# A transformer layer on one Trainium2 core: deferred down products, norm chains in pieces on VectorE, five slabs ahead and three equal token groups

## The chip, the core and the metric

The kernel is one launch on one core of a Trainium2 chip. The core has a matrix engine (TensorE, PE in the profile; PEld are its weight loads), three engines for element work (VectorE, DVE; ScalarE, ACT; GpSimd, POOL) and a queue that starts most transfers (SyncE, SP). Each engine executes its own instructions in the order in which they were written; they wait for one another by semaphores. The metric is the time of one execution on the device in microseconds; the kernel before takes 1278.63 us (median of three runs, 1278.6 to 1278.74).

## The reference, cut to what matters

One layer of a hybrid decoder, float32 in and out, 1024 prompt tokens and 32 sample tokens, T = 1056 columns in all, model width 1024:

```python
h = _rms(x, n_mix_pre)
z = h @ w_in                                   # q, k, v, pooling inputs
a, k_state, v_state = attn_fn(q, k, v)          # sliding window of 128, sinks
m, pool_state = _pool_mixer(u, pool_prev, pos0, w_pool, pool_scale)
mix = jnp.concatenate([a, m], axis=-1) @ w_out
x = x + _rms(mix, n_mix_post)
f = _rms(x, n_ffn_pre)
f = (jax.nn.silu(f @ w_gate) * (f @ w_up)) @ w_down     # D_FF = 2816
x = x + _rms(f, n_ffn_post)
x = x + jax.nn.sigmoid(x @ w_ple_gate) * (p @ w_ple)
```

`_rms(x, g)` is x / sqrt(mean(x*x) + 1e-6) * g over the model width. The states of the caches are outputs too.

## The kernel before

Activations lie transposed: the model width on 128 partitions in 8 pieces (KC), the tokens along the columns. The tokens are cut into three groups g = 0, 1, 2 of `NS` = 384, 384 and 288 columns. A tensor of one group is kept as two halves of 4 pieces (`half`, 128 x 4 x NS[g]).

**Precision by splits.** Each operand of a large product is kept as a high part, cast by ScalarE (`wh`, `fh`, `hid`, `sh`), and the rest, subtracted by VectorE (`wl`, `fl`, `sl`); the function is `split`. A product of one 128 x 128 weight piece is three matmuls: high x high, high x low, low x high (`gemm`). `ops8` is a product over all 8 pieces, so 24 matmuls; `ops4` over 4, so 12. Raw weights come by SP's queue into `wr` tiles (`W_RAW` = 2 buffers), and the split pairs into a ring of `W_PAIRS` = 4 pairs. A tile is reused when TensorE has read it for the last time; a cast that needs it waits for that.

**Stages.** First norm and input projection; pooling and attention, filled up with out-projection products; the rest of the out-projection; then the feed-forward part; then the last stage (`ple_out`), the gate and projection of the per-layer input. The feed-forward width is 22 chunks of 128, two chunks a slab, 11 slabs. For each slab and the groups that take part, `gate_up` makes gate and up of each chunk and puts silu(gate) * up, split, into `hid`; `down` multiplies by the slab's rows of `w_down` and adds to the outputs `o` on VectorE.

**Seven products.** Groups 0 and 1 go together through gate and up by seven products instead of eight, with sums of the weights (`w_sums`: four GpSimd operations and two splits into `sh`, `sl`, called S1 to S4) and sums of the operands (`t_sum`, T1 to T4). Their first two products, of the gate's own weights with B11 and B21, need no sum; the third needs S2. Group 2 takes direct products (`direct`, 24 matmuls each).

**WALK.** It is the list of (slab, groups): `AHEAD` = 3 slabs of group 2 alone, then 8 slabs of all three, then the first 3 slabs of groups 0 and 1 alone. While group 2 works alone, the norms of groups 0 and 1 are made. A group's chain (`ffn_steps`) is: sum of squares over partitions on TensorE (`acc`), root on ScalarE, `dg` on VectorE, a matmul that spreads the factor r over the partitions, y*r on VectorE, x+y on GpSimd, squares on ScalarE, sums of the halves (`sum_halves`) on GpSimd and VectorE, the second norm's factor in the same way, eight scalings by gain and r on VectorE (`scalar_tensor_tensor`), two operand splits. `ple_steps` is the chain behind the last down products. The chains are generators whose three or four parts are called between products at fixed places.

**Order.** TensorE's instructions stand in the order of the code; the downs of a slab follow its two chunks directly. What the other engines do stands in an order that a scheduler makes from the code's order and its own estimates of readiness.

Of the kernel before, what the change touches and what calls it, by code (L numbers as in the profile page):

```python
# [16 lines left out]
P = 128  # L17
# [7 lines left out]
NS = (384, 384, 288)  # L25
OFF = (0, 384, 768, T)
G = 3
NX = max(NS)
# [8 lines left out]
AHEAD = 3  # L37
# [9 lines left out]
W_RAW = 2  # L47


A_SLOTS, B_SLOTS = 20, 7  # L50
# [3 lines left out]
def trunk_kernel(  # L54
# [47 lines left out]
    def big(shape, dt=F32, s="a"):  # L102
        return apool.tile(shape, dt, tag="a", bufs=A_SLOTS, name=nm(s))

    def small(shape, dt=F32, s="b"):
        return apool.tile(shape, dt, tag="b", bufs=B_SLOTS, name=nm(s))

    def half(g, dt=F32, s="h", home=None):
        return (home or (small if g == 2 else big))([P, 4, NS[g]], dt, s)

# [80 lines left out]
    WALK += [(s, (0, 1)) for s in range(AHEAD)]  # L191
    WGU, WD = [], []
    for s, _ in WALK:
        WGU.append([[add_plan(w_gu[c, j], [P, KC, P]) for j in range(2)] for c in range(SLAB * s, SLAB * s + SLAB)])
        WD.append([add_plan(w_dn[s, j], [P, SLAB, 512]) for j in range(2)])
    WPE = []
    for _ in range(2):
        w = []
        for m in range(KC):
            if m % 4 == 0:  # L200
                wp = add_plan(w_ple[m // 4], [P, 2, 512])
            w.append((wp, add_plan(w_pg[m], [P, KC, P])))
        WPE.append(w)

# [16 lines left out]
    def rstd_steps(acc):  # L221
# [4 lines left out]
        w = n // G  # L226
        sm = bank()
        for i in range(G):
            mm(sm[:w, i : i + 1], acc[:, i * w : (i + 1) * w], ones[:, 0:1], start=True, stop=True)
        sd = spool.tile([P, G], F32, tag="sd", name=nm("sd"))  # L230
        se.activation(sd[:w], sm[:w, :G], AF.Sqrt, bias=epst[:w], scale=1.0 / D)
# [4 lines left out]
            ident[:w, :w].unsqueeze(1).to_broadcast([w, G, w]),  # L236
            sd[:w].unsqueeze(2).to_broadcast([w, G, w]),
            op=ALU.mult,
        )
        yield  # L240
# [15 lines left out]
    def sum_halves(sqs, g, eng):  # L256

        a, b = sqs
        eng.tensor_tensor(a, a, b, op=ALU.add)
# [10 lines left out]
    for g in range(G):  # L270
# [19 lines left out]
        acc1.append(sum_halves(sqs, g, ve))  # L290
# [11 lines left out]
    wpl2 = small([P, 2, 4, P], F32R)  # L302
    wplh, wpll = wpl2[:, 0], wpl2[:, 1]
    split(wplh, wpll, wpl)
    sts = big([P, 8 * NDEC * PST + 4 * 16 + 4 * PST])
# [19 lines left out]
    def u_proj(c):  # L325
        w = weights(U0[c])
        ue = big([P, ULEN])
# [17 lines left out]
        two = [big([P, ULEN]) for _ in range(min(2, c + 1))]  # L345
# [30 lines left out]
    qkv = [big([P, T]) for i in range(6)]  # L376
# [11 lines left out]
    misc = big([P, 6, P])  # L388
# [11 lines left out]
    vtok = big([P, NB, P])  # L400
# [599 lines left out]
```

## Time and profile before

| | us |
|---|---|
| median of three runs | 1278.63 |
| profiled execution | 1280.9 |
| its span, first to last instruction | 1279.1 |
| TensorE busy in the span | 1161.9 |
| VectorE / ScalarE / GpSimd busy | 729.3 / 428.0 / 243.6 |
| mean granted clock of TensorE | 0.951 |
| start, to the first uninterrupted work of TensorE | 0 to 57.3 |
| group 2 alone in its first slabs | 305.8 to 446 |
| slabs of all three groups | 446 to 965 |
| slabs of groups 0 and 1 alone | 965 to 1129.6 |
| last downs and turn to the last stage | 1129.6 to 1172.9 |

The clock is the share of full speed that TensorE was granted. A row of a window gives for each engine its busy time and the number of instructions, then that clock, the busy share of the DMA engines and their rate. A row of a group names the line, the engine, the operation, output and inputs, shapes, the count, then busy us and mean ns. A row of waits gives the total, the number and the longest.

### The profile page before, as it was taken

How to read it: one execution, taken by the hardware profiler on the slowest of the kernel's cores; microseconds unless marked ns; L12 is line 12 of the kernel's file. 1: busy time of each engine (PE TensorE's matmuls, PEld its weight loads, DVE VectorE, ACT ScalarE, POOL GpSimd, SP SyncE). 2: the span in 40 equal slices, each digit the busy share in tenths (PEclk: the TensorE clock that was granted, in tenths of full speed). 3: DMA queues.
4: the chain of work that ended last, by engine and by line, in shares of the span. 5: the costliest groups of instructions: out<-in, count | busy, mean ns of one | idle time of the engine just before them, and what ended most of it. 6: DMA issues, size and time to landing. Idle time of an engine off the chain costs nothing.

```text
span 1279.1 us, 17291 instructions
## 1 busy us (share of the span) xinstructions
PE 1161.9 (91%) x7075; PEld 1121.9 (88%) x7075; DVE 729.3 (57%) x1117; ACT 428.0 (33%) x744; POOL 243.6 (19%) x180
## 2 busy tenths in 40 slices
PE   4599998998947799999999999999999798968998
PEld 3499985788946799999999999999999698968998
DVE  7655245753558745364646464656566856597432
ACT  5222045554446324321313132323232322354220
POOL 3343021124450021111111121202021111100000
PEclk8699998998978899999999999999999899987999
DMA  5211120062233212011202021212112112225421
GB/s 202 66 34 61 41 103 18 17 238 84 82 115 99 100 33 67 33 67 34 67 34 66 34 66 34 67 33 67 34 67 79 66 50 66 83 98 183 146 87 44
DMA packets 33375, 94.80 MB, mean 74 GB/s; under 512 B 3956, under 2 KB 14484, under 8 KB 33296
## 3 DMA queue, kind: packets, MB, share of 16 engines
q1 hardware_dynamic: 31536, 91.93, 21.1%
q10 hardware_dynamic: 1760, 1.78, 0.4%
q8 instruction: 55, 0.90, 0.3%
q14 instruction: 24, 0.20, 0.1%
HBM read 83.58 MB, written 10.11 MB: 73 GB/s over the span
## 4 chain that ended last, share of the span: by engine, by line
PE 59%; DVE 7%; issue 1%; ACT 1%; DMA 1%; POOL 0%; DVEq 0%; ACTq 0%; POOLq 0%
PE b L115 59%; DVE fl L145 1%; DVE x L842 1%; DVE wl L145 1%; DVE y L673 1%; DVE acc L565 0%; POOL wr L714 0%; DMA wr<-in_w_dn_dram 0%; DVE sl L145 0%; ACT sh L144 0%; DVE o L839 0%; DVE y L643 0%; ACT wh L144 0%; DVE hid L145 0%; DMA wr<-in_w_gu_dram 0%
## 5 line engine op out<-in xcount | busy, mean ns | idle before, releaser
L115 PE MATMUL b<-hid,wh 128*128 128x384 f32 (+1 forms) x1056 | 258.5, 330 | 25.3 <-ACT hid L144 17.8
L115 PE MATMUL b<-fh,wh 128*128 128x288 f32 (+1 forms) x808 | 257.2, 318 | 0.0
L115 PE MATMUL b<-fh,wl 128*128 128x288 f32 (+1 forms) x808 | 256.2, 317 | 0.0
L115 PE MATMUL b<-fl,wh 128*128 128x288 f32 (+1 forms) x808 | 256.2, 317 | 0.0
L144 ACT CAST wh<-wr 128x1024 fp32r<-128x1024 f32 x128 | 134.0, 1048 | 267.6 <-PE b L115 221.1
L145 DVE TENSOR_TENSOR wl<-wr,wh 128x1024 fp32r<-128x1024 f32 x128 | 172.4, 1348 | 83.0 <-ACT wh L144 83.0
L115 PEld LDWEIGHTS b<-hid,wh 128*128 128x128 f32 x1056 | 189.4, 193 | 29.3 <-ACT hid L144 19.3
L714 POOL TENSOR_TENSOR wr<-wr 128x512 f32<-128x512 f32 x44 | 62.3, 1415 | 599.7 <-DVE wl L145 598.0
L115 PE MATMUL b<-hid,wl 128*128 128x384 f32 (+1 forms) x528 | 172.7, 327 | 1.2 <-DVE wl L145 1.2
L810 DVE TENSOR_TENSOR o<-o,b 128x384 f32<-128x384 f32 (+1 forms) x240 | 121.2, 518 | 63.6 <-PE b L115 62.6
L115 PEld LDWEIGHTS b<-fh,wh 128*128 128x128 f32 x808 | 154.6, 191 | 0.3
L115 PEld LDWEIGHTS b<-fl,wh 128*128 128x128 f32 x808 | 154.4, 191 | 0.3
L115 PEld LDWEIGHTS b<-fh,wl 128*128 128x128 f32 x808 | 154.3, 191 | 0.0
L115 PE MATMUL b<-h,wh 128*128 128x384 f32 (+1 forms) x480 | 119.5, 335 | 17.0 <-ACT wh L144 10.2
L144 ACT CAST sh<-wr 128x1024 fp32r<-128x1024 f32 x44 | 46.0, 1048 | 234.1 <-PE b L115 170.3
L115 PE MATMUL b<-fh,sl 128*128 128x384 f32 x352 | 118.8, 337 | 2.3 <-DVE sl L145 2.3
L115 PE MATMUL b<-fh,sh 128*128 128x384 f32 x352 | 118.7, 337 | 2.2 <-ACT sh L144 2.2
L115 PE MATMUL b<-fl,sh 128*128 128x384 f32 x352 | 118.3, 336 | 0.0
L115 PEld LDWEIGHTS b<-h,wh 128*128 128x128 f32 x480 | 88.1, 198 | 18.1 <-ACT wh L144 10.2
L115 PEld LDWEIGHTS b<-hid,wl 128*128 128x128 f32 x528 | 102.0, 193 | 1.5 <-DVE wl L145 1.5
L145 DVE TENSOR_TENSOR sl<-wr,sh 128x1024 fp32r<-128x1024 f32 x44 | 53.8, 1223 | 74.2 <-ACT sh L144 74.2
L115 PE MATMUL b<-h,wl 128*128 128x384 f32 (+1 forms) x240 | 79.7, 333 | 2.7 <-DVE wl L145 2.7
(157 smaller groups left out, 1658.1 us busy)
## 6 DMA issues: line engine op xcount, KB each, us to landing
wr<-in_w_gu_dram SPq DMA_DIRECT2D x56, 512.0 KB, 3.2
wr<-in_w_dn_dram SPq DMA_DIRECT2D x28, 512.0 KB, 3.2
wr<-in_w_pg_dram SPq DMA_DIRECT2D x16, 512.0 KB, 3.5
wr<-in_w_in_dram SPq DMA_DIRECT2D x10, 512.0 KB, 3.4
wr<-in_w_out_b_dram SPq DMA_DIRECT2D x8, 512.0 KB, 3.3
xr<-in_x_dram SPq DMA_DIRECT2D x4, 768.0 KB, 6.9
wr<-in_w_out_a_dram SPq DMA_DIRECT2D x6, 512.0 KB, 3.2
x<-in_x_dram SPq DMA_DIRECT2D x4, 768.0 KB, 8.6
```

The costliest lines, as they stand in the source:

```text
L115: ins = te.matmul(*args, **kw)
L144: se.copy(hi, src)
L145: ve.tensor_tensor(lo, src, hi.bitcast(F32), op=ALU.subtract)
L673: ve.tensor_tensor(out, a, b, op=ALU.subtract)
L714: ge.tensor_tensor(out, a, b, op=op)
L810: ve.tensor_tensor(o, o, v, op=ALU.add)
L842: ve.scalar_tensor_tensor(xh[:, c, :], yh[:, c, :], gn[:, 3, k : k + 1], xh[:, c, :], op0=ALU.mult, op1=ALU.add)
```

## The change

The token groups become three of 352. The chains get all their additions on VectorE and are cut into smaller pieces; `turn` counts matmuls and lets a chain's next piece out when VectorE should have done the one before (`load / share`). `AHEAD` is 5, so that `WALK` has 5 slabs of group 2, 6 of all groups, 5 of groups 0 and 1. The down products of a slab are issued behind the next slab's first products, and for all groups alternately. The last stage begins with two tiles of group 2 ahead of the last downs. Weights are asked for through one list of items in the order of use (`need`, four items ahead), raw buffers are 3. One pool of 27 slots replaces two of 20 and 7. The attention blocks go 5, 6, 7, 0 to 4 instead of 6, 7, 0 to 5.

```diff
-NS = (384, 384, 288)
-OFF = (0, 384, 768, T)
 G = 3
-NX = max(NS)
+N = T // G
+NS = (N,) * G
+TB = 4
-AHEAD = 3
+AHEAD = 5
+LOOK = 4
-W_RAW = 2
-A_SLOTS, B_SLOTS = 20, 7
+W_RAW = 3
+A_SLOTS = 27
...
+    def need(k, ahead=LOOK):
+        for i in range(len(made), min(k + ahead + 1, len(ITEMS))):
+            kind, js = ITEMS[i]
+            if kind == "direct":
+                w_split(js[0])
+                made[i] = pairs[js[0]]
+            else:
+                made[i] = w_sums(*(raws[ITEMS[j][1][0]] for j in js))
+            for kind, js in ITEMS[i + 1 : i + 3]:
+                if kind == "direct":
+                    w_load(js[0])
+        return made[k]
...
-            eng.tensor_tensor(acc_g, acc_g, sq, op=ALU.add)
+            ve.tensor_tensor(acc_g, acc_g, sq, op=ALU.add)
...
+    def turn(n, share=0.45):
+        now[0] += n
+        for ch in list(chains):
+            while ch in chains and ch[1] <= now[0]:
+                try:
+                    load, wait = next(ch[0])
+                except StopIteration:
+                    chains.remove(ch)
+                    break
+                dve[0] = max(dve[0], now[0]) + load / share
+                ch[1] = dve[0] + wait
...
         for yh, xh in zip(ys[g], x1[g]):
             ve.tensor_tensor(yh, yh, bc4(r), op=ALU.mult)
-            ge.tensor_tensor(xh, xh, yh, op=ALU.add)
+            ve.tensor_tensor(xh, xh, yh, op=ALU.add)
             se.activation(yh, xh, AF.Square)
-        acc2 = sum_halves(ys[g], g, ge)
-        yield
+            yield 20, 0
+        yield 0, 13
+        acc2 = sum_halves(ys[g], g)
+        yield 20, 6
...
+        wg = need(ig)
+        if 0 in gs:
+            p1 = tmp(n, "p1")
+            se.copy(p1, product(quarter(wg, 0), f7["B11"]))
+        if 2 in gs:
+            sl = tmp(n, "sl")
+            se.activation(sl, direct(wg), AF.Silu)
+        if 0 in gs:
+            c11 = tmp(n, "c11")
+            add(c11, p1, product(quarter(wg, 1), f7["B21"]))
+            se.activation(c11, c11, AF.Silu)
+        if pending:
+            pending()
...
+    def downs(n):
+        s, gs = WALK[n]
+        for m in range(KC):
+            for g in (2, 0, 1):
+                if g in gs:
+                    (last_down if g == 2 and s == NSLAB - 1 else down)(n, m, g)
+        if s == NSLAB - 1:
+            chain(ple_steps(2), 19)
     for n, (s, gs) in enumerate(WALK):
...
         for i in range(SLAB):
-            gate_up(*WGU[n][i], i, gs, between)
...
+            gate_up(WGU[n][i], i, gs, (lambda: downs(n - 1)) if i == 0 and n else None)
...
+    for m in range(FIRST):
+        ple_out(0, m, 2)
+    for m in range(KC):
+        last_down(END, m, 0)
+    chain(ple_steps(0), 19)
+    for m in range(KC):
+        last_down(END, m, 1)
+    chain(ple_steps(1), 19)
+    for m in range(FIRST, KC):
+        ple_out(0, m, 2)
```

How this stands in the engines' own orders is shown at three places. The first is VectorE at the end of the out-projection, before slab 0. In these rows y_1263 and y_2531 (before), y_1266 and y_2532 (after) belong to group 0, y_1265 and y_2181 (before), y_1268 and y_2188 (after) to group 2; fl_2606, and in the change fl_2831 and fl_2840, are the low parts of group 2's operands, and dg is what the factor is made from. Before:

```order
L145 TENSOR_TENSOR wl_2525<-wr_2522,wh_2524 128x1024
L232 RECIPROCAL sd_2564<-sd_2564 96x3
L234 TENSOR_TENSOR dg_2567<-c_76,sd_2564 96x288
L643 SCALAR_TENSOR_TENSOR y_1265<-x_2315,c_72,b_2598 128x288 x4
L643 SCALAR_TENSOR_TENSOR y_2181<-x_2317,c_72,b_2598 128x288 x3
L145 TENSOR_TENSOR fl_2606<-y_1265,fh_2605 128x1152
L643 SCALAR_TENSOR_TENSOR y_2181<-x_2317,c_72,b_2598 128x288
```

And in the change:

```order
L277 TENSOR_TENSOR dg_2781<-c_76,sd_2778 88x352
L704 TENSOR_TENSOR y_1266<-y_1266,b_2818 128x1408
L608 TENSOR_TENSOR acc_1303<-acc_1303,sq_2809 128x352
L147 TENSOR_TENSOR wl_2813<-wr_2736,wh_2812 128x1024
L705 TENSOR_TENSOR x_2326<-x_2326,y_1266 128x1408
L716 SCALAR_TENSOR_TENSOR y_1268<-x_2322,c_72,b_2823 128x352 x4
L716 SCALAR_TENSOR_TENSOR y_2188<-x_2324,c_72,b_2823 128x352 x3
L147 TENSOR_TENSOR fl_2831<-y_1268,fh_2830 128x1408
L716 SCALAR_TENSOR_TENSOR y_2188<-x_2324,c_72,b_2823 128x352
L704 TENSOR_TENSOR y_2532<-y_2532,b_2818 128x1408
L147 TENSOR_TENSOR fl_2840<-y_2188,fh_2839 128x1408
L705 TENSOR_TENSOR x_2328<-x_2328,y_2532 128x1408
```

Group 0's y*r and x+y now stand between group 2's second dg and the splits of group 2's operands. On TensorE the two factors stand together at the very end of the out-projection (b_2783 is its last product), right ahead of slab 0:

```order
L117 MATMUL b_2783<-mh_187,wl_2526 128x352
L117 MATMUL b_2818<-dg_2701,c_81 128x352
L117 MATMUL b_2823<-dg_2781,c_81 128x352
L117 MATMUL b_2850<-fh_2830,wh_2685 128x352
L117 MATMUL b_2850<-fl_2831,wh_2685 128x352
```

Before, six out-projection products stood between the factor of group 2 (made from dg_2567) and slab 0.

The second place is ScalarE in a slab of groups 0 and 1 alone, at its second chunk (p is the first product, c becomes silu of the second, sh are the casts of the weight sums):

```order
L829 COPY p_8705<-b_8706 128x352
L836 ACTIVATE c_8720<-c_8720 128x352
L146 CAST sh_8695<-wr_8396 128x1024
L146 CAST sh_8699<-wr_8568 128x1024
L146 CAST wh_8736<-wr_8609 128x1024
L146 CAST wh_8804<-wr_8703 128x1024
L146 CAST hid_8874<-c_8925 128x352
```

The casts of the sums stand behind the activation of c here, and casts of weights for later products ahead of the cast of hid.

The third place is VectorE at the turn to the last stage. Before, group 0's chain (o_4010, o_4011, x_9545, x_9547) stands in one piece ahead of the last adds of group 1's downs (o_4021):

```order
L839 TENSOR_TENSOR o_4011<-o_4011,b_9580 128x1536
L842 SCALAR_TENSOR_TENSOR x_9545<-o_4010,c_72,x_9545 128x384 x4
L842 SCALAR_TENSOR_TENSOR x_9547<-o_4011,c_72,x_9547 128x384 x4
L145 TENSOR_TENSOR fl_9588<-x_9545,fh_9587 128x1536
L145 TENSOR_TENSOR fl_9597<-x_9547,fh_9596 128x1536
L810 TENSOR_TENSOR o_4021<-o_4021,b_9600 128x384
```

In the change, group 0's second split (fl_10131) stands behind pieces of group 1's chain (o_4487, x_9874), weight splits and the output operations of group 2's tiles (sg, yo):

```order
L909 TENSOR_TENSOR o_4487<-o_4487,b_10035 128x1408
L950 TENSOR_TENSOR sg_10042<-sg_10042,b_9992 128x352
L912 SCALAR_TENSOR_TENSOR x_9874<-o_4487,c_72,x_9874 128x352
L147 TENSOR_TENSOR wl_10001<-wr_9942,wh_10000 128x1024
L912 SCALAR_TENSOR_TENSOR x_9874<-o_4487,c_72,x_9874 128x352 x3
L952 TENSOR_TENSOR yo_10045<-sg_10042,x_7656 128x352
L147 TENSOR_TENSOR wl_10057<-wr_9956,wh_10056 128x1024
L950 TENSOR_TENSOR sg_10086<-sg_10086,b_10048 128x352
L147 TENSOR_TENSOR wl_10101<-wr_10004,wh_10100 128x1024
L952 TENSOR_TENSOR yo_10089<-sg_10086,x_7656 128x352
L147 TENSOR_TENSOR fl_10131<-x_9748,fh_10130 128x1408
```

So one chain no longer stands whole ahead of the other's sums; its last piece now stands among later work.

More of the change, by code (lines that the diff above doesn't have):

```diff
@@ L22 @@
 T = SEQ + NDEC * DSEQ
-NS = (384, 384, 288)
-OFF = (0, 384, 768, T)
 G = 3
-NX = max(NS)
+N = T // G
+NS = (N,) * G
+OFF = tuple(N * g for g in range(G + 1))
+NX = N
+TB = 4
 WIN = 128
@@ L344, in u_proj @@
         s = ue
-        two = [big([P, ULEN]) for _ in range(min(2, c + 1))]
+        two = [act_tile([P, ULEN]) for _ in range(min(2, c + 1))]
         for sh in range(c + 1):
@@ L627, in trunk_kernel, with chain, finish @@
     fs = [None, None, []]
+    now, dve = [0.0], [0.0]
+    chains = []
+    def turn(n, share=0.45):
[9 more added lines that the diff above has]
+                ch[1] = dve[0] + wait
+    def chain(steps, wait=0):
+        chains.append([steps, now[0] + wait])
+    def finish(ch_list):
+        for ch in ch_list:
+            for _ in ch[0]:
+                pass
+            chains.remove(ch)
     def ffn_steps(g):
@@ L674, in t_sum @@
         f7[name] = f_operand(out, 0)
-    steps = [ffn_steps(g) for g in range(G)]
-    def step(g):
-        next(steps[g], None)
     pinned[0] = True
+    chain(ffn_steps(2), 19)
     for m in range(4):
-        out_attn(m, 0)
-        out_attn(m, 1)
-        if m in (1, 2):
-            step(2)
+        for g in (0, 1):
+            out_attn(m, g)
+            turn(12)
     for m in range(4, KC):
@@ L690, in trunk_kernel @@
         out_proj(m, 0)
-        if m in (4, 5):
-            step(2)
+        turn(24)
+    chain(ffn_steps(0), 19)
     for m in range(4, KC):
         out_proj(m, 1)
-        if m in (4, 5):
-            step(0)
+        need(0, m - 4)
+        turn(24)
+    chain(ffn_steps(1), 19)
+    finish(chains[:-2])
     hid = [None] * G
```

243 lines of the change are left out of this document (112 added, 131 removed).

## The prediction

> **What bounds the kernel now.** I read the top of the page first, then the span cut at the places where TensorE (PE) stops being continuous.
>
> ```profile
> span 1279.1 us, 17291 instructions
> PE 1161.9 (91%) x7075; PEld 1121.9 (88%) x7075; DVE 729.3 (57%) x1117; ACT 428.0 (33%) x744; POOL 243.6 (19%) x180
> ...
> core 0: us, PE busy (x) PEld busy (x) DVE busy (x) ACT busy (x) POOL busy (x), PEclk, DMA share, GB/s
> 0.00:57.30 57.30, 23.91 (x96) 20.74 (x97) 40.35 (x47) 21.57 (x37) 20.15 (x18) 0.81 0.44 150
> 57.30:305.80 248.50, 240.54 (x1541) 213.71 (x1539) 127.88 (x221) 98.25 (x268) 67.83 (x58) 0.97 0.21 73
> 305.80:446.00 140.20, 99.28 (x598) 96.08 (x598) 89.25 (x98) 65.06 (x86) 36.90 (x17) 0.83 0.28 97
> 446.00:965.00 519.00, 519.00 (x3272) 519.00 (x3273) 287.73 (x472) 143.68 (x217) 91.79 (x68) 1.00 0.15 49
> 965.00:1016.00 51.00, 42.57 (x226) 39.65 (x226) 36.56 (x58) 19.54 (x26) 6.94 (x5) 0.92 0.26 91
> 1016.00:1129.60 113.60, 106.70 (x583) 104.52 (x582) 70.76 (x113) 34.83 (x50) 20.02 (x15) 0.96 0.21 69
> 1129.60:1172.90 43.30, 28.14 (x168) 26.82 (x168) 37.91 (x55) 22.62 (x30) 0.00 (x0) 0.83 0.34 125
> 1172.90:1279.10 106.20, 101.73 (x598) 101.36 (x598) 38.88 (x57) 22.45 (x33) 0.00 (x0) 0.97 0.31 103
> ```
>
> From 446 to 965 us, where all three groups run together, PE is busy for 519.00 of 519 us at full clock: nothing but fewer PE columns can help there. PE is late in four other places: the start, the three slabs of group 2 alone (305.8 to 446), the three slabs of groups 0 and 1 alone (965 to 1129.6), and the end (1129.6 to 1172.9). In each, a second price comes on top of idle time: the granted clock drops (0.83, 0.92, 0.83). I take the cost of a stage as its length minus what its matmuls need at full clock: matmuls busy in it, less half of the time at half clock. From 305.8 to 446 the clock of 0.83 is 34% of the stretch at half clock (1 - 2 x 0.17 at full), some 48 us; if 28 of these fell on busy time they cost 14, and with the 40.9 us idle (140.2 - 99.28) the stage costs about 55 us. From 965 to 1129.6: 15.3 us idle and some 9 of clock, 24. From 1129.6 on: 15.2 idle and, with the start of the last stage, some 9 of clock, 24.
>
> What PE waits for in the second stage:
>
> ```profile
> PE b L115 <- DVE dg L234: 11.9, 2, 10.5
> PE b L115 <- ACT hid L144: 10.3, 2, 9.4
> PE b L115 <- POOL acc L565: 7.3, 1, 7.3
> PE b L115 <- DVE hid L145: 5.9, 2, 5.0
> PE b L115 <- DVE acc L262: 5.5, 1, 5.5
> ```
>
> These are the norms of the three groups and the products' outputs: all pass through VectorE (DVE), with pieces on GpSimd (POOL). DVE is dense there, but not full:
>
> ```profile
> 300.00:425.00 125.00, 85.96 (x500) 82.89 (x499) 77.82 (x84) 60.18 (x78) 42.05 (x19) 0.82 0.27 93
> 340.00:425.00 85.00, 51.48 (x319) 49.11 (x318) 61.61 (x62) 44.90 (x53) 26.38 (x9) 0.79 0.32 110
> ```
>
> That is 62% and 72%. So this stage is bound by a chain through engines, not by one engine's load.
>
> **The change part by part.** The sum is made on the span of 1279.1 us; the profiled execution took 1280.9, and the median is 1278.63, so span and median are taken as equal.
>
> *Columns.* Gate and up of one chunk are seven products of 12 matmuls for groups 0 and 1 (384 columns before) and two of 24 for group 2 (288). All become 352 wide.
>
> ```profile
> 711.54 0.33 PE L115 MATMUL b<-fh,wh 128*128 128x384 f32 x1
> ...
> 713.62 0.29 PE L115 MATMUL b<-fh,wh 128*128 128x288 f32 x1
> ...
> 716.01 0.30 PE L115 MATMUL b<-fh,wh 128*128 128x288 f32 x1
> ```
>
> Twelve of 384 take 2.08 us from start to start (0.1733 each), eighteen of 288 take 2.39 (0.1328); 352 lies at 0.1598 between them. Per chunk 84 x 0.0135 is won and 48 x 0.0270 lost: +0.16 us, and with 22 chunks **+3.6 us**. Elsewhere 384 + 384 + 288 = 3 x 352 and nothing changes.
>
> *From the output projection into the first slab.* Here I expect a new stall. TensorE issues the factors of group 0's first norm and of group 2's second norm together, as the last two matmuls before slab 0, and slab 0 needs group 2's operands at once. On VectorE, which works in order, stand between them: group 0's y*r, an addition to acc, a weight split, group 0's x+y, four scalings of group 2, three more, its first split, one more scaling, y*r of group 0's other half, and then the second split that the products need.
>
> ```profile
> L145 DVE TENSOR_TENSOR wl<-wr,wh 128x1024 fp32r<-128x1024 f32 x128 | 172.4, 1348 | 83.0 <-ACT wh L144 83.0
> L810 DVE TENSOR_TENSOR o<-o,b 128x384 f32<-128x384 f32 x160 | 86.6, 552 | 57.2 <-PE b L115 57.2
> L810 DVE TENSOR_TENSOR o<-o,b 128x288 f32<-128x288 f32 x80 | 34.6, 450 | 6.4 <-PE b L115 5.4
> L145 DVE TENSOR_TENSOR fl<-y,fh 128x1536 fp32r<-128x1536 f32 x7 | 12.1, 1755 | 0.6 <-ACT fh L144 0.6
> L643 DVE SCALAR_TENSOR_TENSOR y<-x,c,b 128x384 f32<-128x384 f32 x16 | 8.7, 608 | 0.0
> L633 DVE TENSOR_TENSOR y<-y,b 128x1536 f32<-128x1536 f32 x4 | 6.8, 1752 | 2.1 <-PE b L115 2.1
> ...
> L634 POOL TENSOR_TENSOR x<-x,y 128x1536 f32<-128x1536 f32 x4 | 15.8, 3970 | 11.3 <-DVE y L633 11.3
> ```
>
> At 352 columns an add comes to 0.52 us (between 0.450 and 0.552), a scaling to 0.57, a piece of 4 x 352 to 1.62. Five pieces (8.1), a split (1.35), an add (0.5) and eight scalings (4.6) are 14.6 us after the factor; the first half product (12 x 0.16 = 1.9) runs meanwhile. So 12.7 us idle and about 1.5 for a cold start: **14 us**. Before, PE waited 5.5 and 7.3 us in this place and at half clock after each, so the new stall is about as long as what it replaces.
>
> *Slabs 0 to 4, group 2 alone.* Five slabs instead of three give the norm chains of groups 0 and 1 room of 128.7 us of PE (five slabs of 4 x 24 + 8 x 6 matmuls at 0.16 are 115, the first 72 of the next slab 11.5, the sums of squares 2), where three slabs at 0.1328 gave 57. The adds x+y, the sums of halves and acc + sq go from GpSimd to VectorE: a 1536-wide add took 3.97 us on GpSimd and takes 1.62 there. DVE's work from the factor of group 2 to the last T operand: 27 weight splits 36.4, four y*r and four x+y 13.0, 24 scalings 13.7, nine operand splits 14.6, half sums 6.0, four T differences 6.5, 24 adds of downs 12.4, group 2's own products and splits 9.4, rstd 2.1, together 114 us. It has 128.7 + 14 = 143 us, so it must be 80% dense. Downs now stand behind the next slab's first product (24 x 0.16 = 3.8 us), which covers the hid casts that PE waited 10.3 and 5.9 us for. What remains I put at 4 us, the norm factors (dg) that come a little late at their place in the order. Stage cost 14 + 4 = 18 instead of 55 to 57: **-38 us**. If the cover were gone, the hid waits of 16 us and their clock would be back.
>
> Two more slab passes (16 instead of 14) mean 12 more weight loads, casts and splits; DVE's share of them is in the 114, and the DMA engines were 27% busy in this stage: no price.
>
> *Slabs of groups 0 and 1 alone, now five.* Before:
>
> ```profile
> PE b L115 <- ACT hid L144: 7.4, 3, 4.3
> PE b L115 <- DVE sl L145: 2.3, 4, 0.6
> PE b L115 <- ACT sh L144: 2.2, 3, 0.9
> ...
> 1103.40 1.04 ACT L144 CAST sh<-wr 128x1024 fp32r<-128x1024 f32 x1 [6.34 <-PE b L115]
> 1104.36 0.52 ACT L791 ACTIVATE p<-p 128x384 f32<-128x384 f32 x1
> ...
> 1104.50 0.45 PE L115 MATMUL b<-fh,sh 128*128 128x384 f32 x1 [0.92 <-ACT sh L144]
> ...
> 1106.80:1110.30 3.50, 3.50 (x13) 3.50 (x12) 2.32 (x5) 1.57 (x2) 0.00 (x0) 0.51 0.82 277
> ```
>
> The hid waits at the downs (7.4 us, and half clock after the longer) are now behind two products of 12 matmuls, 3.8 us: gone. The wait for sh and sl in the second chunk (0.92 + 0.64 in the last slab) comes back in each of five slabs and grows: ScalarE (ACT) now has the activation of c11 ahead of the sh cast, so an add (0.52) and an activation (0.5) come on top: 2.6 us, five times, 13. Of three such waits before, one was followed by 3.5 us at a clock of 0.51 (last row), which costs 1.75; longer waits should do so more often, so two or three in five, 4. With 2 us of remainder 19 against 24: **-5 us**.
>
> A page bears on the clock. The Trainium skill, TensorE: Matmul & The Clock Gate, section HAM oscillation, gives the rule that TensorE should have no idle gaps above about 3.4 us, since such a gap crosses a window and the clock is halved. The row of 0.51 speaks against it as a limit from below: two waits of 0.92 and 0.64 us came before it. By the rule alone the 4 us of clock in this stage would not be there, and the sum would be 4 us less.
>
> *The end.*
>
> ```profile
> PE b L115 <- DVE acc L565: 10.0, 2, 9.5
> PE b L115 <- DVE wl L145: 5.1, 1, 5.1
> ```
>
> Before, group 0's whole chain (two y*r, eight scalings, two splits, some 12 us) stands on VectorE ahead of the last adds of group 1's downs, and the 9.5 us are PE's wait for the sum behind it; the 5.1 are a weight split behind group 1's chain. Now two tiles of group 2 come ahead of the last downs, six stand behind them, and the chains are cut in pieces between the adds: both waits go. Late next is group 0's second operand. It stands behind group 1's y*r, four scalings, three weight splits and four output operations, with its own split 11.7 us of DVE after group 1's factor, while PE has 12.5 us of products (two tiles of 30 matmuls and 18 more) before it wants it. By the rows that just does; but the output operations and a weight split ahead of it wait in their turn for the products of those last tiles, so that the queue can't run through. I make it 6 us late (the length of one tile and an operation), group 1's second operand another 4 us, and 3 for the clock: 13 instead of 24: **-11 us**.
>
> *Start and attention.* Equal groups change the loads of x and a third raw buffer puts x loads behind waiting weight loads on SP; the long wait there is this one:
>
> ```profile
> PE b L115 <- DVE dg L234: 13.7, 3, 11.4
> ...
> xr<-in_x_dram SPq DMA_DIRECT2D x4, 768.0 KB, 6.9
> ```
>
> At best half of 11.4 goes (-6), at worst one x load's time is added (+7). I take 0, since the order of loads and norms stays. A block of attention now straddles two groups twice: two more pieces, +1.
>
> **Sum:** 1279.1 + 3.6 - 38 - 5 - 11 + 1 = **1230 us**.
>
> **Rivals.**
>
> *VectorE's queue becomes the bound of slabs 0 to 4.* For: 80% is wanted and 72% was reached between 340 and 425; moved adds lie in its order. Against: part of what kept it idle there was GpSimd's 3.97 us links, now gone. At 72%, 114 us take 158 instead of 143: +15, **1245**; at the 62% of 300 to 425, 184: +41, 1271.
>
> *The stalls shrink more than I think.* If the 14 us at the first slab are halved (the factor of group 0 ready early, its pieces done before group 2's factor comes), the (0,1) slabs lose only what they did per slab (1.55 us and a third of 1.75, 11 us in all), and the start gains its 6: 1230 - 7 - 8 - 6 = **1209**. For it speaks that group 0's factor rests on older sums; against it that both factors are issued after the last product.
>
> *Look-ahead casts block ScalarE (the other side).* Each need of a weight now casts up to four items ahead, and a cast that waits for a pair which PE still reads stands ahead of the activations and hid casts behind it. If all 22 chunks with seven products had the stall of 1103.40 and its half clock (1.55 + 1.75), not only the second chunks of the last five slabs, 17 x 3.3 = 56 come on top: **1286**, slower. It decides from 15 of these 17 chunks on (49 us). Against: sh casts waited for PE in the middle stage too, while PE was busy all of its 519.00 us, for group 2's direct products of 24 matmuls stood behind.
>
> *The change doesn't do what it says:* downs are deferred but hid is late all the same, or two groups' chains collide: that is in the first rival's range.
>
> **How the numbers follow.** Forecast 0.62 (its own range 1219 to 1240), VectorE's queue 0.20, smaller stalls 0.13, blocked ScalarE 0.05. The 80% range reaches to the first rival's 1245 and some way towards 1271, and to 1209 on the other side: 1208 to 1252. This kernel's runs differ by 0.14 us, and 0.2% (2.6 us) is about what can be told from no change. Only the last rival ends above 1276: slower 0.04, same 0.02, faster 0.94.
>
> **What would show it.** The window of the first slab: PE idle for 12 to 13 us with a wait for group 2's fl, and no wait for acc or hid L144 in the five slabs; DVE 75% dense or more there. PE busy without a gap through the six slabs of three groups. Five stalls of 2 to 3 us ended by sh in the last slabs. A wait of about 6 us for fl before the last stage. I would be wrong if PE had waits for hid or silu in the six middle slabs, if the five first slabs took over 150 us, or if the start moved by more than 8.

## The result

The changed kernel takes 1226.05 us (median of four runs, 1224.97 to 1226.42), the kernel before beside it 1278.68. The ratio is 0.958, with a 95% interval of 0.957 to 0.960: 4.1% faster. The forecast was 1230 in a range of 1208 to 1252. The profiled execution took 1225.98 us, its span is 1223.9.

The top of the page, and the span cut at the places that answer to those shown of before:

```profile
span 1223.9 us, 17417 instructions
PE 1147.9 (94%) x7099; PEld 1109.0 (91%) x7099; DVE 741.7 (61%) x1161; ACT 433.3 (35%) x755; POOL 187.1 (15%) x150
...
0.00:56.10 56.10, 27.27 (x101) 22.07 (x101) 39.98 (x47) 21.62 (x37) 18.39 (x18) 0.77 0.47 162
56.10:332.50 276.40, 268.61 (x1731) 242.93 (x1731) 145.21 (x257) 111.82 (x294) 50.97 (x44) 0.99 0.22 76
332.50:345.00 12.50, 3.91 (x13) 3.53 (x13) 12.50 (x15) 4.67 (x5) 0.00 (x0) 0.69 0.26 100
345.00:460.00 115.00, 113.96 (x712) 112.59 (x711) 93.78 (x117) 60.13 (x75) 0.68 (x1) 0.99 0.41 138
460.00:870.00 410.00, 410.00 (x2585) 409.78 (x2584) 226.53 (x376) 116.15 (x178) 72.27 (x55) 1.00 0.16 54
870.00:905.00 35.00, 23.77 (x124) 21.70 (x124) 28.15 (x38) 14.82 (x19) 7.50 (x6) 0.80 0.23 76
905.00:1100.00 195.00, 186.67 (x1153) 184.33 (x1152) 128.25 (x214) 67.40 (x95) 37.24 (x28) 0.99 0.24 77
1100.00:1136.60 36.60, 36.60 (x231) 35.86 (x229) 35.09 (x55) 22.10 (x31) 0.00 (x0) 1.00 0.66 236
1136.60:1223.90 87.30, 77.13 (x462) 76.19 (x461) 32.17 (x48) 14.58 (x23) 0.00 (x0) 0.95 0.19 63
```

The stage in which group 2 works alone (332.5 to 460) has become nearly whole: after a hole of 8.6 us ahead of slab 0, TensorE is busy for 113.96 of 115 us at a clock of 0.99, where before 40.9 of 140 us were idle at 0.83. (The stretch of before, 305.8 to 446 us, begins with the last products of the output projection: slab 0 starts at 346.1 us there, and of the idle time the first 5.5 us lie ahead of it.) VectorE is busy for 93.78 of those 115 us, 82%. What PE still waits for, in the first slabs, in the last five slabs, and at the turn to the last stage:

```profile
PE b L117 <- ACT fh L146: 7.6, 1, 7.6
PE b L117 <- DVE hid L147: 1.0, 2, 0.7
PE b L117 <- DVE fl L147: 1.0, 1, 1.0
...
PE b L117 <- ACT hid L146: 8.0, 2, 6.1
PE b L117 <- ACT sh L146: 6.6, 5, 1.4
PE b L117 <- DVE sl L147: 3.3, 5, 0.7
PE b L117 <- DVE hid L147: 1.6, 2, 1.2
...
PE b L117 <- ACT fh L146: 3.2, 1, 3.2
PE b L117 <- DVE fl L147: 2.3, 2, 1.2
```

The waits for acc and the two long ones for hid of the first slabs are gone, as forecast; so are those for dg, for which the forecast had kept 4 us. In their place stand one wait for group 2's operands (fh), the sh and sl waits, five times, and one that the forecast did not have: 9.6 us for hid, casts on ScalarE (8.0) and splits on VectorE (1.6), in the first slab of groups 0 and 1 alone.

### The profile page after: what moved, and what is told of

Same layout as the page of the kernel before. It is cut to its first block, busy times and chain, and to the rows that moved or that the text cites. A ratio compares the mean times of both kernels' runs of the same rounds, so it can differ in the third digit from the quotient of the medians.

```text
span 1223.9 us, 17417 instructions
## 1 busy us (share of the span) xinstructions
PE 1147.9 (94%) x7099; PEld 1109.0 (91%) x7099; DVE 741.7 (61%) x1161; ACT 433.3 (35%) x755; POOL 187.1 (15%) x150
## 4 chain that ended last, share of the span: by engine, by line
PE 83%; DVE 8%; POOL 3%; ACT 3%; DMA 1%; issue 1%; POOLq 0%; SPq 0%; DVEq 0%; ACTq 0%
PE b L117 79%; POOL wr L790 3%; DVE wl L147 2%; PE b L541 1%; PE b L509 1%; DMA xr<-in_x_dram 1%; ACT wh L146 1%; DVE h L324 1%; DVE sl L147 1%; ACT a L483 1%; ACT sh L146 1%; DVE fl L147 1%; DVE y L716 0%; PE b L588 0%; DVE x L912 0%
## 5 line engine op out<-in xcount | busy, mean ns | idle before, releaser
L117 PE MATMUL b<-fh,wh 128*128 128x352 f32 x808 | 263.9, 327 | 10.8 <-ACT fh L146 10.8
L117 PE MATMUL b<-hid,wh 128*128 128x352 f32 x1056 | 255.7, 324 | 10.7 <-ACT hid L146 8.0
L117 PE MATMUL b<-fl,wh 128*128 128x352 f32 x808 | 261.4, 324 | 3.3 <-DVE fl L147 3.3
L117 PE MATMUL b<-fh,wl 128*128 128x352 f32 x808 | 261.2, 323 | 0.0
L117 PE MATMUL b<-hid,wl 128*128 128x352 f32 x528 | 170.1, 322 | 0.0
L880 DVE TENSOR_TENSOR o<-o,b 128x352 f32<-128x352 f32 x240 | 116.0, 515 | 43.0 <-PE b L117 42.9
L117 PE MATMUL b<-h,wh 128*128 128x352 f32 x480 | 123.7, 340 | 18.6 <-ACT wh L146 9.7
L117 PE MATMUL b<-fh,sh 128*128 128x352 f32 x352 | 114.8, 326 | 6.6 <-ACT sh L146 6.6
L117 PE MATMUL b<-fh,sl 128*128 128x352 f32 x352 | 114.0, 324 | 3.3 <-DVE sl L147 3.3
L117 PE MATMUL b<-fl,sh 128*128 128x352 f32 x352 | 113.5, 322 | 0.0
```

The source lines that it names most:

```text
L117: ins = te.matmul(*args, **kw)
L880: ve.tensor_tensor(o, o, v, op=ALU.add)
```

## The experiments

The kernel before, run beside them, had medians of 1278.70, 1279.52, 1280.62 and 1278.87 us in the four sessions, with single runs between 1272.9 and 1281.5; so a few us between two medians are read by stage, from the profiles.

**The deferral taken out.** The edit:

```diff
-            gate_up(WGU[n][i], i, gs, (lambda: downs(n - 1)) if i == 0 and n else None)
+            gate_up(WGU[n][i], i, gs, None)
+        if n < END:
+            downs(n)
```

(with the down weights asked for in that order, and group 2's eight products first).

> The changed kernel with one part undone: every slab's down products stand directly behind its own two chunks again, group 2's eight first (the last slab's downs stay where the change has them). Theory (deferral covers the chain silu, product, hid cast, hid split): each of the five slabs of group 2 alone gets about 3 us of waiting for hid back, each of the slabs of groups 0 and 1 alone about 2.5, and half clock behind some of them, 8 in all: about 35 us more, 1250 to 1270. Rival (five slabs ahead and the lighter GpSimd have made hid early anyway, the deferral covers nothing): 1224 to 1232, with no waits for hid in the five first slabs.

Measured: 1274.69 us (ratio to before 0.9965, 0.9943 to 0.9986). The rest of the change without the deferral is worth 4 us (2 to 7 by the interval). The waits of the first five slabs, those of the last slabs, and the clock behind two of the latter:

```profile
PE b L117 <- DVE hid L147: 8.1, 5, 3.6
...
PE b L117 <- ACT hid L146: 6.2, 5, 2.2
...
PE b L117 <- ACT hid L146: 19.0, 5, 8.8
...
1033.00:1037.00 4.00, 4.00 (x20) 4.00 (x20) 1.57 (x4) 0.00 (x0) 0.37 (x1) 0.72 0.00 0
...
1085.00:1089.00 4.00, 4.00 (x23) 4.00 (x22) 1.72 (x4) 0.00 (x0) 0.26 (x1) 0.82 0.00 0
```

Waits for hid of 1.8 to 3.6 us are back in each of the first five slabs. Among the last slabs four have them: 3.6 us in three, 9.9 us in the first. The kind is as expected; the expected 35 us were too low, for it is 48.6. Up to the first wait for sh the kernel is 28.9 us later than the changed one (900.97 against 872.06), and from there to the wait ahead of the last stage another 21.4 (285.9 against 264.6). Only some 13 and 14 us of that are new idle time; much of the rest is clock, for each of the three waits of 3.0 us was followed by half clock (0.72 and 0.82 are the means of 4 us that begin some 3 us behind the end of two of them; the 4 us after that are at 1.00).

**The deferral alone**, on the kernel before:

```diff
-            gate_up(*WGU[n][i], i, gs, between)
+            gate_up(*WGU[n][i], i, gs, between, (lambda: downs(n - 1)) if i == 0 and n else None)
```

> The kernel before with one part of the change alone: a slab's down products stand behind the next slab's first gate products; groups, GpSimd's additions, three slabs ahead and the chains are those of before. Theory (the deferral is worth by itself the waits for hid of before, 16 us in the three slabs of group 2 and 9 in the last three slabs, and some of their clock): 1240 to 1260. Rival (it needs the room of the rest: here the chains keep VectorE full up to the end of the third slab, so that PE waits for the operands of groups 0 and 1 instead): 1265 to 1282.

Measured: 1277.22 us against 1279.52 (0.998, 0.9963 to 0.9997): the rival. Between 340 and 440 us PE waits for this:

```profile
PE b L115 <- DVE wl L145: 16.2, 1, 16.2
PE b L115 <- DVE dg L234: 11.9, 2, 10.5
PE b L115 <- POOL acc L565: 7.3, 1, 7.3
```

The waits for dg and acc are those of before. No hid any more, but 16.2 us for a weight split. VectorE's timeline there shows why:

```profile
409.74 0.45 DVE L766 TENSOR_TENSOR sl<-sl,b 128x288 f32<-128x288 f32 x1
410.10 1.75 DVE L673 TENSOR_TENSOR y<-y,y 128x1536 f32<-128x1536 f32 x1
411.77 3.42 DVE L145 TENSOR_TENSOR fl<-y,fh 128x1536 fp32r<-128x1536 f32 x2
415.11 1.75 DVE L673 TENSOR_TENSOR y<-y,y 128x1536 f32<-128x1536 f32 x1
416.77 0.45 DVE L145 TENSOR_TENSOR hid<-sl,hid 128x288 fp32r<-128x288 f32 x1
417.14 1.22 DVE L145 TENSOR_TENSOR wl<-wr,wh 128x1024 fp32r<-128x1024 f32 x1
```

The remains of groups 0 and 1's chains (T differences and their splits) are put out in one piece at the end of the third slab and stand ahead of both hid's split and the next weight split. With the downs in their old place PE stood at the first, with the downs deferred it stands at the second, for 16.2 us (before: 9.4 and 5.0 us for hid). So the deferral needs the rest of the change, and the rest needs the deferral: 2 and 4 us each alone, 53 together. Which part of the rest it needs this run does not show. It is not mainly the two more slabs: the next run has the deferral without them and is still 41 us below the kernel before. The chains in pieces (`turn`), the list of weights with a third raw buffer and the new end were not taken out one by one.

**Three slabs ahead instead of five**, the rest as changed (`AHEAD = 3`):

> The changed kernel with three slabs of group 2 ahead instead of five, so 3, 8 and 3 slabs as before the change. Theory (the two more slabs are the room for VectorE's work on the norms of groups 0 and 1): about 86 us of VectorE work at 80% want 107 us, three slabs give about 81, so 26 us more there, and two slabs of groups 0 and 1 fewer give 8 back: about 1243 (1235 to 1255). Rival (the pieces and the deferral did it, the room is not needed): 1212 to 1222, faster by the two slabs' stalls.

Measured: 1237.51 us, 11.5 more than the changed kernel. One new wait carries it, at 425.4 to 436.6 us in the first slab of all groups, and two of the slabs of groups 0 and 1 alone, with their sh waits, are gone. The wait, and the row of VectorE's timeline that ends it:

```profile
PE b L117 <- DVE c L824: 11.2, 1, 11.2
...
436.04 0.52 DVE L824 TENSOR_TENSOR c<-p,b 128x352 f32<-128x352 f32 x1
```

The wait stands among the deferred downs. Seven of them have run, and the eighth wants a bank (a place for a product's output, 8 in the kernel's `psum` pool) that the addition c has yet to read; from 421 to 436 us the operand work of groups 0 and 1 (y, fl) and two splits of weight sums stand ahead of c on VectorE. So the deferral covers a late VectorE only as far as there are free banks. The two extra slabs are that room; the expectation of 17 us more was of the right kind, and the 11.5 measured are a third less.

**The additions back on GpSimd:**

```diff
-            ve.tensor_tensor(xh, xh, yh, op=ALU.add)
+            ge.tensor_tensor(xh, xh, yh, op=ALU.add)
-        acc2 = sum_halves(ys[g], g)
+        acc2 = sum_halves(ys[g], g, ge)
```

(and the additions of squares in the output projection).

> The changed kernel with x+y, the first sum of halves and the additions of squares of the output projection back on GpSimd. Theory (they are links of chains, 3.97 against 1.62 us each): the wait ahead of slab 0 grows from 7.6 us by some 4 to 8 us, the other links lie in slabs with room: 1229 to 1236. Rival A (VectorE's queue is what is short at that place, so taking work off it helps): 1216 to 1224. Rival B (the chains are the bound of the first five slabs as well): each of four more chain parts later by 5 us, 1240 and more.

Measured: 1226.55 and 1235.91 us, a median of 1231.23; the span is 1224.8 in the profile of the first, 0.9 longer than the changed kernel's. In the profile the wait ahead of slab 0 is 8.4 us instead of 7.6 and a wait for hid 1.8 instead of 0.3; no other wait moves by more than 1 us. The two runs are too far apart to give the median a sign, and what made the second one longer is open. By the profile this part is worth about 1 us, less than the theory's 4 to 8; the rival that VectorE gains is not seen either.

**Equal groups alone**, on the kernel before (`NS = (352, 352, 352)`, four blocks of 88 for the factor, the changed order of attention blocks):

> The kernel before with only the groups changed to three of 352 (norm factors from four blocks of 88, attention blocks in the changed order, all else as before). Theory (columns): 22 chunks times 0.16 us more of TensorE, +3.6, and the last slabs of groups 0 and 1 have a little less to do for VectorE: 1280 to 1284, the slabs of all groups at full clock longer by 1.3 us. Rival (group 2's larger share covers more in its own three slabs): three slabs of 144 matmuls at 0.160 instead of 0.133 give 11.7 us more cover, so a few us faster than before, 1268 to 1276.

Measured: 1279.27 us against 1278.70 (1.002, 0.9996 to 1.0045), not to be told from no change, nor from the 3.6 us expected. The stretch from the last wait of the third slab to the first wait for sh, first of before, then of this kernel:

```profile
445.90:991.20 545.30, 545.26 (x3424) 544.79 (x3424) 301.93 (x496) 151.22 (x228) 97.31 (x72) 1.00 0.16 52
```

```profile
444.70:994.30 549.60, 549.56 (x3426) 548.99 (x3426) 300.23 (x496) 151.35 (x228) 96.95 (x72) 1.00 0.16 52
```

With the same work at full clock it is 4.3 us longer. The formula of the forecast gives 2.6 for these 16 chunks and 1.1 for the wider downs of group 2's third slab, 3.7. So the columns cost about what was said. In this profile (1275.48 us, one of the shorter runs of 1274.7 to 1286.5) the waits around them took it back; that they do so in every run is not shown.

**Group 0's first chain begun later** (`chain(ffn_steps(0), 110)` for 19):

> The changed kernel with group 0's first norm chain begun about 96 matmuls later, so that on VectorE its y*r and x+y no longer stand between group 2's second factor and group 2's operands. Theory (they are 3 of the 8 us that the first operand is late): the wait ahead of slab 0 falls from 8.6 to 4 us or less, and the later chains of groups 0 and 1 still end in time within five slabs: 1218 to 1223. Rival (five slabs have no 15 us to spare): a new wait of 5 us or more ahead of the first slab of all groups, 1225 to 1240.

Measured: 1226.47 us. The wait ahead of slab 0 falls from 8.6 to 6.1 us, so group 0's pieces on VectorE are 2.5 us of it (3 were expected); and a wait of 2.9 us for hid appears at 363 to 367, where the chains of groups 0 and 1 now start together. No net gain.

**T4's product ahead of S2's:**

```diff
+        p4 = product(quarter(wu, 1), f7["T4"])
         s = need(is_)
         add(p1, p1, product(s["S2"], f7["T2"]))
...
-        add(c21, u3, product(quarter(wu, 1), f7["T4"]))
+        add(c21, u3, p4)
```

> The changed kernel with the product of the up weights with T4 put ahead of the product S2 with T2 in each chunk of groups 0 and 1 (same seven products, its result stays in its bank until u3 is there). Theory (in the last five slabs PE waits 2.1 us in every second chunk because the up pair's tile comes free late, then cast, split, four GpSimd sums and the sh cast follow in a row; T4 earlier frees the pair 3.8 us sooner and stands as 1.9 us of cover ahead of S2): waits for sh and sl shrink from 9.9 to under 2, 1212 to 1220. Rival (c11's activation ahead of sh on ScalarE is what makes sh late, as the prediction had it): the wait moves with the products and shrinks by the 1.9 us of cover only where it is shorter than that, sh stays late by what c11 takes, 1222 to 1227.

Measured: 1209.94 us (0.946, 0.943 to 0.949), 16 less than the changed kernel. All waits for sh and sl are gone (9.9 us and 1.7 of clock); the late hid is 1.2 us shorter, and the rest lies within the spread of this kernel's runs (1207.53 to 1213.87). What is left from the first slab of groups 0 and 1 to the last stage:

```profile
PE b L117 <- ACT hid L146: 6.6, 2, 3.4
PE b L117 <- DVE hid L147: 1.8, 2, 1.2
```

The edit does two things: it frees the up weights' pair sooner, and it puts 1.9 us of cover ahead of S2's product. ScalarE's timeline of this run tells them apart, in the second chunk of the first slab of groups 0 and 1:

```profile
921.72 2.00 ACT L146 CAST sh<-wr 128x1024 fp32r<-128x1024 f32 x2 [2.14 <-POOL wr L790]
```

The first of these casts ends at 922.8 us, 3.9 us before PE's product with S2 (926.7); in the changed kernel it ends 1.4 us after PE wants it. Of the 5.3 us gained the cover is 1.9. So the wait came from the up weights' pair, as the theory of this run had it. The changed kernel's own timelines of ScalarE, VectorE and GpSimd show the chain in a second chunk:

```profile
921.84 1.05 ACT L146 CAST wh<-wr 128x1024 fp32r<-128x1024 f32 x1 [4.67 <-PE b L117]
...
929.89 1.04 ACT L146 CAST sh<-wr 128x1024 fp32r<-128x1024 f32 x1 [6.27 <-POOL wr L790]
```

```profile
922.96 1.22 DVE L147 TENSOR_TENSOR wl<-wr,wh 128x1024 fp32r<-128x1024 f32 x1
```

```profile
924.31 1.46 POOL L790 TENSOR_TENSOR wr<-wr 128x512 f32<-128x512 f32 x1 [29.12 <-DVE wl L147]
...
928.58 1.28 POOL L790 TENSOR_TENSOR wr<-wr 128x512 f32<-128x512 f32 x1
```

The cast of the up weights waits until PE has finished with a pair of the ring (4.67 us), then come its split, four sums on GpSimd (5.5 us) and the cast of sh, which ends 1.4 us after PE wants it.

**The late hid in the first slab of groups 0 and 1.** Three runs went at these 9.6 us. First the chain behind group 2's last downs paced slower (`share` 0.2 from there on):

> The changed kernel with the chain behind group 2's last downs paced slower (its pieces further apart, share 0.2 instead of 0.45 from the first slab of groups 0 and 1 alone on). Theory (the 9.6 us of waits for hid at 888 to 901 come from VectorE: two pieces of that chain delay a weight split, this GpSimd's sums, these the sh cast, and the hid cast behind it on ScalarE): those waits fall to under 3 us and the cold clock behind them goes, 1212 to 1220. Rival (the wait belongs to the first slab without group 2, whose weights and sums are asked for too late whatever the chain does): the waits stay at 8 to 10 us, 1223 to 1228.

Measured: 1229.76 us; the waits are 7.9 us, at the same place. The first pieces of the chain still fall into that slab, so the run leaves the theory open rather than refutes it. Then, on top of T4 first, the casts of sh and hid on ScalarE kept in the code's order:

> T4 first, and on ScalarE the casts of the weight sums (sh) and of hid kept in the order in which the code issues them, so that the sh cast of the next slab's sums no longer stands ahead of the hid cast that the downs want. Theory (the wait for hid in the first slab of groups 0 and 1 alone, 7.8 us there with T4 first, is ScalarE held by an sh cast that waits for GpSimd): the waits for hid there fall under 3 us, 1201 to 1207 against 1210 with T4 first alone. Rival (the wait is VectorE's: its pieces of the chain beside GpSimd's sums take 2 to 3 times as long and u times p comes late whatever ScalarE does): 5 us and more of waits stay, 1207 to 1212. The fixed order may also hold casts back in the slabs of all groups; then PE has waits there.

Measured: 1217.25 us, 7 more than T4 first; hid is waited for 8.0 us there (8.4 with T4 first alone). ScalarE's order was not the cause. Part of the 7 us are new waits for hid that the fixed order brings elsewhere, 2.7 us of them at 366 to 369, where it was 0.3. VectorE's timeline in this kernel shows what is:

```profile
891.14 1.44 DVE L915 SCALAR_TENSOR_TENSOR x<-o,c,x 128x352 f32<-128x352 f32 x1
892.51 1.58 DVE L857 TENSOR_TENSOR c<-c,c 128x352 f32<-128x352 f32 x1
...
895.53 2.09 DVE L915 SCALAR_TENSOR_TENSOR x<-o,c,x 128x352 f32<-128x352 f32 x2
...
899.05 1.63 DVE L149 TENSOR_TENSOR fl<-x,fh 128x1408 fp32r<-128x1408 f32 x1
900.59 0.52 DVE L864 TENSOR_TENSOR u<-u,p 128x352 f32<-128x352 f32 x1
```

The chain's pieces (L915, fl) stand ahead of the products c (L857) and u (L864) that hid is made from, and while GpSimd works on its sums (890.94 to 896.7 in this run) x and c take 1.0 to 1.6 us each instead of 0.52 to 0.58. Last, the chain begun one slab later, in a kernel with the edits of the next paragraph too (`if n == NSLAB: chain(ple_steps(2), 19)`):

> The kernel t4hp1 (1203) with two edits: the chain behind group 2's last downs begins one slab later, and no tile of group 2 stands ahead of the last downs. Theory for the first (what keeps hid late at that place, 7.8 us, is VectorE: the chain's pieces stand ahead of the operations that hid needs, while GpSimd's sums of weights make VectorE's two-input operations 2 to 3 times as long): with the chain elsewhere under 2 us of waits are left there; a slab later the products hide it, for VectorE was 66% busy there. Second: the 3.0 us of waits for operands at the end go under 1, but the last hid has no cover but its own order, up to 2 us. Together 1190 to 1196. Rival (that slab is the first whose weights come without group 2's products to hide them, so the wait stays or moves to the next slab with the chain): 1198 to 1204.

There the waits for hid in the first such slab are gone and 8.3 us of them stand in the second, at 923 to 934: they follow the chain. That the chain on VectorE is the cause is shown; that a later slab hides it, as expected, is not so.

**Towards a faster kernel.** T4 first, group 0's chain later, the chains paced twice as fast in the output projection (`share` 0.9), one tile of group 2 ahead of the last downs:

> T4 first, group 0's first chain begun later as before, group 2's chain paced twice as fast during the output projection (share 0.9), and one tile of group 2 ahead of the last downs instead of two. Theory for the place ahead of slab 0 (the second factor of group 2 is issued only after the last product because the chain is paced too slowly): with its factor some 70 matmuls earlier the wait of 8.6 us falls under 2. Theory for the end (group 0's second operand and group 1's come late by the 5.6 us that PE waits there; one more tile of group 2 behind the last downs is 4.8 us of cover): under 2 us of waits, and hid of the last slab still in time behind one tile. Together 1210 less 8 to 14: 1196 to 1203. Rival (the wait moves on: the last hid, or the operands of groups 0 and 1 at the first slab of all groups): 1204 to 1212 with a new wait at one of these two places.

Measured: 1202.91 us (0.940, 0.938 to 0.941). The wait ahead of slab 0 is 1.9 us instead of 8.6, for group 2's factor is issued two products of 24 matmuls ahead of the end of the output projection; the end keeps 3.0 us of waits for operands, and 2.9 us for hid stand at 357 to 360. The kernel of the paragraph above, with no tile of group 2 ahead of the last downs, has no wait of PE at the turn to the last stage and took **1196.79 us** (1195.77 to 1197.74; 0.936, 0.934 to 0.938), the fastest here, 29 us below the changed kernel.

Its sister, with that one tile and group 1's chain begun later:

> As best2, but with one tile of group 2 ahead of the last downs, and group 1's first chain begun 41 matmuls later. Theory: the 2.9 us of waits for hid at 357 to 360 come from group 1's and group 0's y*r and x+y following each other on VectorE ahead of hid's split; apart they leave under 1 us. End as in t4hp1, 3.0 us. 1191 to 1197, within 2 of best2. Rival (group 1 is then late for the first slab of all groups): a new wait of 3 us or more there, 1196 to 1205.

Measured: 1206.03 us. The later chain did not take away the wait for hid at 355 to 359 (4.0 us instead of 2.9). In its trace other pieces of group 0's chain stand ahead of hid there, its squares on ScalarE (355.64 us) and a sum of halves on VectorE (357.05 us); which of them holds it was not tested. And the end has its 3.2 us of waits again.

## Why the prediction was right, and where not

The time lay 4 us under the forecast, from terms of both signs. The large term was right: the first slabs cost 12.8 us of idle time and clock where 18 were forecast, against some 52 before. Of the others the last slabs are 5 us over, the end 5 and the start 1 us under. That errors of 5 us and opposite sign cancel is luck.

- **Columns, +3.6.** Right: 4.3 where 3.7 was due in the stretch above.
- **Ahead of slab 0, 14.** The place and the cause were right, the size a little high: 7.6 and 1.0 us idle and about 3 of clock, 12 in all. VectorE's timeline of the changed kernel:

```profile
331.96 1.62 DVE L704 TENSOR_TENSOR y<-y,b 128x1408 f32<-128x1408 f32 x1 [1.87 <-PE b L117]
...
335.07 1.62 DVE L705 TENSOR_TENSOR x<-x,y 128x1408 f32<-128x1408 f32 x1
336.61 3.52 DVE L716 SCALAR_TENSOR_TENSOR y<-x,c,b 128x352 f32<-128x352 f32 x7
340.08 1.62 DVE L147 TENSOR_TENSOR fl<-y,fh 128x1408 fp32r<-128x1408 f32 x1
...
343.65 1.62 DVE L147 TENSOR_TENSOR fl<-y,fh 128x1408 fp32r<-128x1408 f32 x1
```

  The order is the one foreseen, and from the factor to the end of the second split it takes 13.3 us (14.6 foreseen). But PE does not stand until then: the first operand lets it start at 340.1, and at half clock its first twelve matmuls last until the second is there. The sum took 12.7 us of idle time and 1.5 of clock; the half clock stretched the first twelve matmuls, and so part of it lay under the wait for the second operand. The run with group 0's chain begun later shows that its pieces are 2.5 us of the 8.6; the run with the faster pace as well shows that the late factor is 4.2 more.
- **Slabs 0 to 4, 4 us left.** 1.0 measured behind slab 0's start, for hid and not for dg; VectorE is 82% busy where 80% was foreseen. The 72% seen before was no limit of the queue.
- **The cover.** The text says that without it the hid waits of 16 us and their clock would be back. Up to the first wait for sh it was 28.9 us, in the whole kernel 49. The sum, which prices the parts one after the other, does not show that the deferral and the rest are worth only 2 and 4 us without each other.
- **Slabs of groups 0 and 1, 19.** 19.6 us idle and some 4.6 of clock, 24, so no gain over before in the stage; its parts were wrong. "The hid waits at the downs are gone" failed: 9.6 us are there once, because the chain behind group 2's downs fills VectorE in that slab. The sh waits were priced 13 and are 9.9, by the wrong reason: c11's activation is ahead of sh in the first chunk of a slab, where the downs cover it. The rows of ScalarE shown with the change as those of the second chunk are the first chunk's; in the second, sh at 929.9 us stands ahead of it. And the 4 us of clock behind five such waits are 1.7: only after the fifth did it fall, for 3.4 us. By the limit of about 3.4 us for a gap that the Trainium skill, TensorE: Matmul & The Clock Gate, section HAM oscillation, gives, the term would be 0, which is nearer here; but the fall behind the fifth wait, and those behind the waits of 3.0 us in the run without the deferral, speak against it as a limit.
- **The end, 13.** 5.6 us idle and about 3 of clock. The place was right; group 0's second operand came 1.2 us late where 6 were forecast, group 1's 4.4 (3.2 and 1.1) where 4 were, so it is the first of the two terms that was too large.
- **The start, 0.** 1.2 us less.

Of the rivals, VectorE's queue as the bound of the first slabs is refuted: PE is busy for 113.96 of 115 us there while VectorE is at 82%. The smaller stalls did not come either: 12 us ahead of slab 0 and not 7, 24 in the last slabs and not 11, and the start gave 1 us of 6. The other side, ScalarE blocked in all chunks, is refuted by the 410.00 us of 410 in the middle; the pair that comes free late, its first link, is real in five of the chunks.

## What to carry to other kernels

A wait that ends on a product's output can be covered by putting other products ahead, but only if what they need doesn't stand in the same queue behind the same piece of work; so check the second waiter of that queue before counting the cover. It also reaches only as far as there are free banks: seven products in the run with three slabs ahead. Undo one part and do one part alone: the deferral and the rest of the change, worth 2 and 4 us each, were worth 53 together, and no sum of separate terms shows that. Where a ring of tiles feeds a long row of engines, look at the last use of each tile: moving one earlier by two products was worth 16 us here.

## What the runs showed that was not expected

Waits of 3.0 us halved the clock for some 3.4 us each time (three of three in the run without deferral); two waits of 1.4 and 0.7 us close together did so once in four in the changed kernel. In each of the profiles the clock changes only at places that lie a multiple of 3.41 us apart. Cut at these places, the third and the fourth pair of waits look like this, each with the 4 us behind it:

```profile
1019.91:1023.32 3.41, 1.98 (x11) 1.69 (x11) 2.67 (x3) 3.37 (x6) 0.00 (x0) 1.00 0.16 25
1021.90:1026.00 4.10, 4.07 (x25) 4.07 (x26) 4.00 (x7) 2.34 (x5) 0.00 (x0) 1.00 0.66 188
...
1064.28:1067.69 3.41, 1.75 (x9) 1.46 (x10) 2.44 (x3) 3.37 (x6) 0.00 (x0) 1.00 0.09 14
1066.50:1070.00 3.50, 3.47 (x15) 3.47 (x16) 3.50 (x6) 2.34 (x5) 0.00 (x0) 0.67 0.62 167
```

The gaps are alike, but not their place. Only the fourth pair lies nearly whole in one such piece, with 1.66 us idle (3.41 less 1.75); the others are cut in two, with 1.44, 1.21 and 1.43 us idle in the worse piece. The other profiles fit that: from 300 us on, a piece at full clock with more than 1.8 us idle was followed by half clock each time, one with less than 1.49 never, and between the two both occur. No run moved a gap on purpose to test it.

While GpSimd works on the weight sums, VectorE's operations whose inputs are both tiles (x, c and u by p) took up to 1.6 us instead of 0.5 to 0.6; those that read a product's bank (p and c with b) kept their 0.51 to 0.52. With the norm's additions off GpSimd this is left, in the feed-forward part, only beside those sums.
